# The first modulation's partial sum on VectorE: its place among the differences, and five blocks instead of four

## The chip, the core and the metric

The kernel runs on one core of one Trainium2 chip. A core has TensorE (PE: matmuls, with weight loads listed as PEld), VectorE (DVE), ScalarE (ACT), GpSimd (POOL) and SyncE (SP), which issues most of the transfers. Each has its own queue of instructions, which it takes in order, and they meet at semaphores. The metric is the device time of one execution in microseconds (us), the median of several runs.

## What is computed

A trunk of two layers for one sequence of 2048 positions and 1024 channels, all in float32. What matters here is the front of layer 0, the modulation of the input and the first product:

```
cond = silu(c)                                   # (1, 1024)
mod = cond @ ada_w[0] + ada_b[0]                 # ada_w[0]: (1024, 3072)
shift, scale, gate = split(mod, 3)
u = x * (1 + scale) + shift                      # x: (2048, 1024)
a, g, z = split(u @ w_in + b_in, 3)              # then a gated convolution, a second
                                                 # product, and a residual LayerNorm
```

Layer 1 is built alike, with another mixer. The output is (1, 2048, 1024).

## The kernel before, in words

The sequence is cut into halves of 1024 positions, and each product of a half is made as two by two blocks by a Strassen-Winograd scheme: seven products of blocks instead of eight, for which differences of the blocks of `u` are needed: `t1` to `t4` beside the blocks `b11`, `b21`, `b22` themselves (`b12` enters only through differences). For accuracy each of these seven is kept as two tiles, a rounded one made by ScalarE (`...h`, line L219) and the rest that the rounding left (`...l`, L220), made by GpSimd, and for `t1` and `t4` by VectorE. The weights (`wa`, `wz`, from the raw blocks `rawa`, `rawz`) are split in the same way by ScalarE and GpSimd. A product is then three matmuls for each of four sets of channels.

The 1024 channels are handled as four **sets** of 2 x 128 channels at the start. The loop at L971 runs over them, i from 0 to 3 (and once more, for the last products). A set does the following:

- `modulation_a(i)` (L443) loads eight blocks of `ada_w`, 128 rows each, `adak` (j = 0 to 5, in `u` buffers) and `adal` (j = 6 and 7, in a `raw` buffer, of which there are four, shared with the raw weights). VectorE multiplies block 0 by its entry of `cond` (L456) and adds blocks 1 to 3 to it, one scalar_tensor_tensor each (L458): the **sum**. TensorE then makes the modulation `pm`: for each of four outputs, blocks 4 to 7 against `cond`, and at last the sum against a column of ones. VectorE adds the bias (L470, tile `mod`).
- `u_block` (four times) loads a block of `x` (`xkua`), TensorE transposes it (`ptxua`), and ScalarE applies scale and shift as it copies it out of PSUM (L236, tile `ufua`).
- `u_parts` makes the seven pairs of tiles. VectorE's part are four differences (L253) and the rests of `t1` and `t4`.
- `first_products` runs, with the set before, the four products that open the kernel's long sequence: three of weight pair 0, one of weight pair 1. After set 0 the first three parts of pair 0 are asked for.

Who goes first: a planner orders each engine's queue when the kernel is built, by priorities and its own estimate of times. Instructions in an `urgent` block have a high priority, others go by their place in the program. Two orders are fixed by hand: TensorE's instructions stay in program order (`keep_in_program_order` ties an instruction behind the one traced before it on its engine), and a load stays behind the last load of weights or of `ada_w` (chain "w") and of its own chain. VectorE's instructions are not tied. What follows the start, some 1600 us of it, is one sequence of products with convolution steps of VectorE and GpSimd laid between them.

Of the kernel before, what the change touches and what calls it, by code (L numbers as in the profile page):

```python
# [9 lines left out]
F32 = mybir.dt.float32  # L10
F32R = mybir.dt.float32r
AF = mybir.ActivationFunctionType
ALU = mybir.AluOpType
# [3 lines left out]
P = 128  # L17
D = 1024
S = 2048
K = D // P  # L20
KH = K // 2
# [18 lines left out]
def hybrid_trunk(ctx, tc, x, c, ada_w, ada_b, a_w_in, a_b_in, a_conv_w, a_conv_b,  # L40
# [7 lines left out]
    nc = tc.nc  # L48
# [7 lines left out]
    def st(tag, shape, name, dtype=F32):  # L56
        return sb.tile(shape, dtype, tag=tag, bufs=BUFS[tag], name=name)

    def bank(tag, name):
        return psum.tile([P, T], F32, tag=tag, bufs=BANKS[tag], name=name)  # L60
# [3 lines left out]
    def load(dst, src, chain="w"):  # L64


        with ExitStack() as order:
            for key in {"w", chain}:
                if key in chains:
                    order.enter_context(tc.issue_after(chains[key]))  # L70
            chains[chain] = nc.sync.dma_start(dst, src).ins
# [25 lines left out]
    def matmul(*args, **kw):  # L97
        return tc.keep_in_program_order(nc.tensor.matmul(*args, **kw))  # L98

    def transpose(*args):  # L100
        return tc.keep_in_program_order(nc.tensor.transpose(*args))  # L101

    clock = [0]
    waiting = []

# [6 lines left out]
    def tick(taps, *gens):  # L112
# [8 lines left out]
        for job in due:  # L121
# [5 lines left out]
    ones = const.tile([P, P], F32, name="ones")  # L127
# [10 lines left out]
    second = [("ada_b1", cols(ada_b[1]), 3 * K),  # L138
              ("b_in", cols(a_b_in[0]), 3 * K),
              ("conv_b", cols(a_conv_b[0]), K),  # L140
              ("ln_g", cols(a_ln_g[0]), K),
              ("ln_b", cols(a_ln_b[0]), K),
              ("post_g", cols(post_ln_g[0]), K),
              ("post_b", cols(post_ln_b[0]), K),
              ("wb", b_conv_w[0].rearrange("k (j p) -> (k j) p", p=P), KB * K)]
# [9 lines left out]
    rows_in = {}  # L155

    def load_rows(gi, g):
        rt = st("acc", [P, P], f"rt{gi}")
        o = 0
        for key, ap, m in g:  # L160
            load(rt[o:o + m, :], ap)
            o += m
        return rt
# [14 lines left out]
    cond = const.tile([P, K], F32, name="cond")  # L178
# [33 lines left out]
    quarters = lambda ap: ap.rearrange("(s m two) d -> s two m d", s=2, two=2)  # L212
# [4 lines left out]

    def split(src, hi, lo, eng=None):
        nc.scalar.copy(hi, src)  # L219
        (eng or nc.gpsimd).tensor_tensor(lo, src, hi.bitcast(F32), op=ALU.subtract)  # L220

    def u_tile(src, name, eng=None):
        hi = st("u", [P, T], name + "h", F32R)
        lo = st("u", [P, T], name + "l", F32R)
        split(src, hi, lo, eng)
        return hi, lo
# [3 lines left out]
    def u_columns(xk, hf, k, su, bu, name):  # L230
        pt = bank("tp", f"ptx{name}{hf}_{k}")
        for t in range(NT):
            transpose(pt[:, t * P:(t + 1) * P], xk[:, t], ident)
        f = st("uf", [P, T], f"uf{name}{hf}_{k}")
        with urgent():
            nc.scalar.activation(f, pt, AF.Identity, scale=su(k), bias=bu(k))  # L236
        return f

    def u_block(src, sc, hf, k, su, bu, name, tag):

        xk = st(tag, [P, NT, P], f"xk{name}{hf}_{k}")
        load(xk, quarters(src)[sc, hf][:, k * P:(k + 1) * P]
             .rearrange("(t p) j -> p t j", p=P), "u")
        return u_columns(xk, hf, k, su, bu, name)

    def u_first(U, fs, name):
        with urgent():
# [2 lines left out]

    def u_second(U, f0, f1, name):
        (b11, b21), (b12, b22) = f0, f1
        tt = lambda o, a, b: nc.vector.tensor_tensor(o, a, b, op=ALU.subtract)  # L253
        with urgent():
            tt(b11, b12, b11)
            U["t1"].append(u_tile(b11, name + "t1", nc.vector))
            U["b22"].append(u_tile(b22, name + "b22"))
            tt(b11, b22, b11)
            U["t2"].append(u_tile(b11, name + "t2"))
            tt(b12, b22, b12)  # L260
            U["t3"].append(u_tile(b12, name + "t3"))
            t4 = st("uf", [P, T], f"{name}t4")
            tt(t4, b21, b11)
            U["t4"].append(u_tile(t4, name + "t4", nc.vector))
# [151 lines left out]
    def product(pair, p, ks=range(KH)):  # L416
        for i in ks:
            pair.mm(p, i)
            if i == KH - 1:
                pair.evacuate(p)  # L420
# [15 lines left out]
    mod0 = const.tile([P, KH, 2, 2], F32, name="mod0")  # L436
    su0 = lambda k: mod0[:, k // 2, 1, k % 2:k % 2 + 1]
    bu0 = lambda k: mod0[:, k // 2, 0, k % 2:k % 2 + 1]
    ab0 = const.tile([P, 2, K], F32, name="ab0")
    nc.vector.tensor_copy(ab0[:, 0], col["ada_b0"][:, :K])  # L440
    nc.vector.tensor_scalar(ab0[:, 1], col["ada_b0"][:, K:2 * K], 1.0, None, op0=ALU.add)

    def modulation_a(i):  # L443

        pm = bank("conv", f"pm{i}")
        raws = []
        last = st("raw", [P, 2, 2, 2 * P], f"adal{i}")
        for j in range(K):
            raw = last[:, j - 6] if j > 5 else st("u", [P, 2, 2 * P], f"adak{i}_{j}")
            load(raw, ada_w[0, j * P:(j + 1) * P, :2 * D].rearrange("p (m d) -> p m d", m=2)  # L450
                 [:, :, 2 * i * P:(2 * i + 2) * P])
            raws.append(raw)

        acc = raws[0]
        with urgent():
            nc.vector.tensor_scalar(acc, acc, cond[:, :1], None, op0=ALU.mult)  # L456
            for j in range(1, 4):
                nc.vector.scalar_tensor_tensor(out=acc, in0=raws[j], scalar=cond[:, j:j + 1],  # L458
                                               in1=acc, op0=ALU.mult, op1=ALU.add)
        for m in range(2):  # L460
            for b in range(2):
                o = m * 2 + b
                for j in range(4, K):
                    matmul(pm[:, o:o + 1], raws[j][:, m, b * P:(b + 1) * P],
                           cond[:, j:j + 1], start=(j == 4), stop=False)
                matmul(pm[:, o:o + 1], acc[:, m, b * P:(b + 1) * P], ones[:, :1],
                       start=False, stop=True)
        with urgent():
            for m in range(2):
                nc.vector.tensor_tensor(mod0[:, i, m], pm[:, 2 * m:2 * m + 2],  # L470
                                        ab0[:, m, 2 * i:2 * i + 2], op=ALU.add)

    sh1 = const.tile([P, K], F32, name="sh1")
    sc1 = const.tile([P, K], F32, name="sc1")
# [482 lines left out]
    def u_parts(U, f0, f1, name):  # L957
        u_first(U, f0, name)
        u_second(U, f0, f1, name)
# [6 lines left out]
    def first_products(pairs, ks):  # L966
        for k in ks:
            for p, r in early:
                product(pairs[p], r, [k])

    for i in range(KH + 1):  # L971
        if i < KH:
            if i == 2:
                rows_in[1] = load_rows(1, second)
            if i == 3:
                rows_in[2] = load_rows(2, taps_1)
                rows_in[3] = load_rows(3, taps_2)
            modulation_a(i)
            fs = [[u_block(x, 0, hf, 2 * i + b, su0, bu0, "ua0", "ta") for b in range(2)]
                  for hf in range(2)]  # L980
            u_parts(US[0, 0], *fs, f"ua0{i}")
        if i == 0:
            for p in (1, 2, 5):
                pa[0][0].part(p)
        if i == 3:
            load_columns(1, second, second_columns)
            nc.vector.tensor_scalar(half_b[:, 0], col["b_in"][:, :K], 0.5, None, op0=ALU.mult)
            nc.vector.tensor_scalar(half_b[:, 1], col["b_in"][:, K:2 * K], 0.5, None,
                                    op0=ALU.mult)
            nc.vector.tensor_scalar(negb, col["conv_b"], -1.0, None, op0=ALU.mult)  # L990
        if i == 4:
            tap_tables()
        if i:
            first_products(pa[0], [i - 1])

    def slowly(gen, ticks=2):
        due = 0
        for _ in gen:
            due += ticks
            while due >= 1:  # L1000
                yield
                due -= 1
# [31 lines left out]
    def second_u():  # L1034

        for i in range(KH):
            f0, f1 = [], []
            for b in range(2):
                for hf, fs in ((0, f0), (1, f1)):
                    fs.append(u_block(x, 1, hf, 2 * i + b, su0, bu0, "ua1", "xk"))  # L1040
                    if hf == 0 or b == 0:
                        yield
            u_parts(US[0, 1], f0, f1, f"ua1{i}")
            yield
# [9 lines left out]
    for n, (p, r) in enumerate(order_a):  # L1054
# [5 lines left out]
        if (p, r) in ((late_b, 3), (late_a, 4)):  # L1060
            k = 0 if r == 3 else 1
# [45 lines left out]
    def ending(pairs, order, rate, q, *beside):  # L1107
# [12 lines left out]
        for gen in gens:  # L1120
            for _ in gen:
# [12 lines left out]
    start = [(0, 1), (0, 2), (1, 1), (1, 2), (2, 1), (2, 2), (0, 5), (0, 6), (0, 3), (0, 7),  # L1134
             (1, 5), (0, 4), (1, 6)]
# [63 lines left out]
```

## Time and profile before

| | |
|---|---|
| median of three runs | 1720.44 us |
| lowest and highest | 1716.67 and 1728.08 us |
| the profiled execution, its own time | 1725.78 us |
| its span on the core | 1724.0 us |
| TensorE busy in the span | 1578.9 us (92%) |
| VectorE, GpSimd, ScalarE busy | 1165.1, 956.8, 665.9 us |

The profile is one execution. Times in it count from the start of the span. A row of the instructions in order of time has start, duration, engine, line, operation, output and inputs; "x3" says that three went into the row, and the bracket at its end says how long the engine had stood idle before it and who ended that. The granted clock of TensorE is given as a share of its full clock: 1.00 is 2.4 GHz and 0.50 is 1.2 GHz.

### The profile page before, as it was taken

To read this page: it belongs to the slowest core of one execution; us is meant where nothing else is said; L and a number is where in the kernel's file an instruction comes from. 1 tells how busy PE (TensorE), PEld (TensorE's weight loads), DVE (VectorE), ACT (ScalarE), POOL (GpSimd) and SP (SyncE) were. 2 spreads that over 40 slices of the span, in tenths; PEclk is the share of its full clock that TensorE was granted. 3 is DMA by queue.
4 is the path that set the end of the run, shared out by engine and by line. 5 is a ranking of instruction groups with operands and counts; after the bars stand their busy time and mean duration, and the time that the engine had idled before them with its cause. 6 is when DMAs were issued, how large, how long until landed. Compare 5 with 4: busy or idle time off the path is not lost.

```text
span 1724.0 us, 20944 instructions
## 1 busy us (share of the span) xinstructions
PE 1578.9 (92%) x6860; PEld 1278.1 (74%) x6860; DVE 1165.1 (68%) x1816; ACT 665.9 (39%) x1134; POOL 956.8 (56%) x808
## 2 busy tenths in 40 slices
PE   4699999889999989868999999898899999999996
PEld 3577787668888767656777887677688888878885
DVE  4438999997899887997999963564832222226555
ACT  2345444655533335373444333333732221112221
POOL 4368886965656343866888776727565541121110
PEclk9799999899999989988999999899899999999998
DMA  7358888779999997634777667986688887787995
GB/s 221 114 198 295 293 298 322 228 276 391 333 354 363 357 368 257 208 147 166 265 266 255 245 245 286 342 289 223 220 294 282 306 298 221 229 299 260 329 336 222
DMA packets 237916, 469.64 MB, mean 272 GB/s; under 512 B 20328, under 2 KB 102640, under 8 KB 237808
## 3 DMA queue, kind: packets, MB, share of 16 engines
q1 hardware_dynamic: 190864, 323.06, 55.6%
q10 hardware_dynamic: 46944, 145.25, 21.7%
q8 instruction: 55, 0.90, 0.2%
q14 instruction: 53, 0.43, 0.1%
HBM read 297.72 MB, written 170.52 MB: 272 GB/s over the span
## 4 chain that ended last, share of the span: by engine, by line
PE 59%; DVE 18%; DMA 11%; issue 4%; POOL 3%; ACT 3%; SPq 1%; ACTq 0%; DVEq 0%; POOLq 0%
PE po L98 17%; PE pxb L98 7%; PE pxc L98 7%; PE pxa L98 5%; PE pzb L98 4%; DVE pca L555 4%; PE pzc L98 4%; PE pza L98 3%; DVE pcb L555 3%; DMA keptb<-wb 3%; PE pxz L98 2%; DMA wr<-w_dram 2%; DMA kepta<-wa 2%; PE pya L98 2%; PE pyb L98 2%
## 5 line engine op out<-in xcount | busy, mean ns | idle before, releaser
L555 DVE SCALAR_TENSOR_TENSOR pcb<-h,w,pcb 128x512 f32<-128x512 f32 x224 | 166.7, 744 | 8.4 <-ACT pcb L563 8.0
L555 DVE SCALAR_TENSOR_TENSOR pca<-h,w,pca 128x512 f32<-128x512 f32 x192 | 142.8, 744 | 0.2
L555 DVE SCALAR_TENSOR_TENSOR pca<-xs,w,pca 128x512 f32<-128x512 f32 x128 | 95.5, 746 | 0.8
L825 DVE TENSOR_TENSOR r<-po,r 128x512 f32<-128x512 f32 x64 | 43.3, 683 | 70.0 <-PE po L98 31.6
L555 DVE SCALAR_TENSOR_TENSOR pcd<-xs,w,pcd 128x512 f32<-128x512 f32 x112 | 83.4, 745 | 0.1
L500 POOL TENSOR_TENSOR ada<-ada,adaw 128x512 f32<-128x512 f32 x48 | 63.9, 1331 | 35.1 <-ACT adaw L494 16.0
L795 ACT ACTIVATE r<-r,nb,rs 128x512 f32<-128x512 f32 x64 | 47.3, 808 | 80.4 <-DVE nb L792 80.3
L220 POOL TENSOR_TENSOR gb_0l<-vb,gb_0h 128x512 fp32r<-128x512 f32 x4 | 5.2, 1295 | 110.2 <-ACT gb_0h L219 110.2
L530 POOL TENSOR_TENSOR wf<-wf,grow 128x512 f32<-128x512 f32 x32 | 41.9, 1318 | 37.6 <-DMA wf<-in_b_w_out_dram 33.6
L832 POOL TENSOR_TENSOR rs<-rs,mhalf 128x1 f32<-128x1 f32 x32 | 18.3, 584 | 75.6 <-DVE rs L831 75.6
L220 POOL TENSOR_TENSOR wa<-rawa,wa 128x512 fp32r<-128x512 f32 x32 | 43.2, 1352 | 21.2 <-ACT wa L219 21.0
L569 POOL TENSOR_TENSOR lead<-lead,part 128x512 f32<-128x512 f32 x32 | 43.6, 1362 | 19.8 <-ACT part L568 17.3
L220 POOL TENSOR_TENSOR wc<-rawc,wc 128x512 fp32r<-128x512 f32 x32 | 46.0, 1437 | 15.5 <-ACT wc L219 15.3
L894 POOL TENSOR_TENSOR hb1c<-c12c,c22c 128x512 f32<-128x512 f32 x16 | 21.1, 1322 | 59.1 <-DVE c22c L392 54.8
L220 POOL TENSOR_TENSOR wf<-wf 128x512 fp32r<-128x512 f32 x32 | 43.0, 1351 | 18.4 <-ACT wf L219 13.7
L804 DVE TENSOR_TENSOR r<-r,g 128x512 f32<-128x512 f32 x48 | 39.6, 838 | 20.0 <-PE ptx L101 17.5
L786 POOL TENSOR_TENSOR r<-r,gb 128x512 f32<-128x512 f32 x32 | 43.9, 1388 | 15.7 <-DMA r<-in_x_dram 14.4
L817 ACT ACTIVATE ub<-ptx,post_sh,post_sc 128x128 f32<-128x128 f32 x128 | 47.0, 482 | 13.4 <-PE ptx L101 13.4
L494 ACT ACTIVATE adaw<-adaw,cond 128x512 f32<-128x512 f32 x64 | 42.5, 715 | 24.8 <-DMA adaw<-in_ada_w_dram 24.3
L220 POOL TENSOR_TENSOR wb<-rawb,wb 128x512 fp32r<-128x512 f32 x32 | 45.2, 1412 | 7.6 <-ACT wb L219 7.4
L220 POOL TENSOR_TENSOR wb<-sb,wb 128x512 fp32r<-128x512 f32 x24 | 35.4, 1473 | 25.0 <-ACT wb L219 25.0
L739 ACT ACTIVATE v<-v,second_columns 128x512 f32<-128x512 f32 x32 | 25.9, 814 | 55.0 <-DVE v L738 53.8
(1388 smaller groups left out, 5589.2 us busy)
## 6 DMA issues: line engine op xcount, KB each, us to landing
wr<-w_dram SPq DMA_DIRECT2D x128, 512.0 KB
kepta<-wa ACTq DMA_DIRECT2D x56, 512.0 KB
wa<-kepta SPq DMA_DIRECT2D x56, 512.0 KB
keptc<-wc ACTq DMA_DIRECT2D x56, 512.0 KB
keptb<-wb ACTq DMA_DIRECT2D x56, 512.0 KB
wc<-keptc SPq DMA_DIRECT2D x56, 512.0 KB
wb<-keptb SPq DMA_DIRECT2D x56, 512.0 KB
adaw<-in_ada_w_dram SPq DMA_DIRECT2D x32, 512.0 KB
```

Source lines behind the costliest of these rows:

```text
L98: return tc.keep_in_program_order(nc.tensor.matmul(*args, **kw))
L220: (eng or nc.gpsimd).tensor_tensor(lo, src, hi.bitcast(F32), op=ALU.subtract)
L494: nc.scalar.activation(raw[:, j], raw[:, j], AF.Identity, scale=cond[:, kk + j:kk + j + 1])
L500: nc.gpsimd.tensor_tensor(acc, acc, raw[:, j], op=ALU.add)
L530: nc.gpsimd.tensor_tensor(w[:, 1], w[:, 1], grow, op=ALU.mult)
L555: nc.vector.scalar_tensor_tensor(out=tiles[out], in0=src, scalar=w, in1=tiles[acc], op0=ALU.mult, op1=op)
L569: nc.gpsimd.tensor_tensor(lead, lead, part, op=ALU.add)
L786: nc.gpsimd.tensor_tensor(rt, rt, gb[0][h], op=ALU.add)
L795: nc.scalar.activation(rts[t, h], rts[t, h], AF.Identity, scale=rs, bias=nb)
L804: eng.tensor_tensor(r, r, g[h], op=ALU.mult)
L817: nc.scalar.activation(fs[k][:, t * P:(t + 1) * P], pt[:, j * P:(j + 1) * P], AF.Identity, scale=post_sc[:, k:k + 1], bias=post_sh[:, k:k ...
L825: nc.vector.tensor_tensor(r, pss[t], r, op=ALU.add)
```

## The change

The loads and the sum of a set leave `modulation_a` for a function of their own, `modulation_loads`. Set 0's is called ahead of the loop; in trip i of the loop, the loads and the sum of set i+1 come after the modulation of set i and the loads of its `x` blocks, and in front of the transposes, copies and differences of set i. While `starting` holds, VectorE's instructions of the sum, the modulation, the differences and the rests of `t1` and `t4` are tied in program order (`pinned`). So VectorE's order becomes: modulation i, sum i+1, differences i, modulation i+1. The sum takes five blocks instead of four (`SPLIT`), and TensorE's part three instead of four. As the loads of set i+1 are now asked for before the weights that follow set i in the program, they also go ahead of these in SyncE's queue. The small row loads (`second`, `taps_1`, `taps_2`) move with them by one trip.

```diff
+    def pinned(made):
+        return tc.keep_in_program_order(made) if starting[0] else made
+
+    starting = [True]
...
     def split(src, hi, lo, eng=None):
         nc.scalar.copy(hi, src)
-        (eng or nc.gpsimd).tensor_tensor(lo, src, hi.bitcast(F32), op=ALU.subtract)
+        made = (eng or nc.gpsimd).tensor_tensor(lo, src, hi.bitcast(F32), op=ALU.subtract)
+        if eng is nc.vector:
+            pinned(made)
...
-    def u_block(src, sc, hf, k, su, bu, name, tag):
+    def x_block(sc, hf, k, name, tag):
 
         xk = st(tag, [P, NT, P], f"xk{name}{hf}_{k}")
-        load(xk, quarters(src)[sc, hf][:, k * P:(k + 1) * P]
+        load(xk, quarters(x)[sc, hf][:, k * P:(k + 1) * P]
              .rearrange("(t p) j -> p t j", p=P), "u")
-        return u_columns(xk, hf, k, su, bu, name)
+        return xk
+
+    def u_block(sc, hf, k, su, bu, name, tag):
+
+        return u_columns(x_block(sc, hf, k, name, tag), hf, k, su, bu, name)
...
-        tt = lambda o, a, b: nc.vector.tensor_tensor(o, a, b, op=ALU.subtract)
+        tt = lambda o, a, b: pinned(nc.vector.tensor_tensor(o, a, b, op=ALU.subtract))
...
-    def modulation_a(i):
-
-        pm = bank("conv", f"pm{i}")
+    SPLIT = 5
+
+    def modulation_loads(i):
+
         raws = []
...
         acc = raws[0]
         with urgent():
-            nc.vector.tensor_scalar(acc, acc, cond[:, :1], None, op0=ALU.mult)
-            for j in range(1, 4):
-                nc.vector.scalar_tensor_tensor(out=acc, in0=raws[j], scalar=cond[:, j:j + 1],
-                                               in1=acc, op0=ALU.mult, op1=ALU.add)
+            pinned(nc.vector.tensor_scalar(acc, acc, cond[:, :1], None, op0=ALU.mult))
+            for j in range(1, SPLIT):
+                pinned(nc.vector.scalar_tensor_tensor(out=acc, in0=raws[j],
+                                                      scalar=cond[:, j:j + 1], in1=acc,
+                                                      op0=ALU.mult, op1=ALU.add))
+        return raws
+
+    def modulation_a(i, raws):
+
+        pm = bank("conv", f"pm{i}")
         for m in range(2):
             for b in range(2):
                 o = m * 2 + b
-                for j in range(4, K):
+                for j in range(SPLIT, K):
                     matmul(pm[:, o:o + 1], raws[j][:, m, b * P:(b + 1) * P],
-                           cond[:, j:j + 1], start=(j == 4), stop=False)
-                matmul(pm[:, o:o + 1], acc[:, m, b * P:(b + 1) * P], ones[:, :1],
+                           cond[:, j:j + 1], start=(j == SPLIT), stop=False)
+                matmul(pm[:, o:o + 1], raws[0][:, m, b * P:(b + 1) * P], ones[:, :1],
                        start=False, stop=True)
         with urgent():
             for m in range(2):
-                nc.vector.tensor_tensor(mod0[:, i, m], pm[:, 2 * m:2 * m + 2],
-                                        ab0[:, m, 2 * i:2 * i + 2], op=ALU.add)
+                pinned(nc.vector.tensor_tensor(mod0[:, i, m], pm[:, 2 * m:2 * m + 2],
+                                               ab0[:, m, 2 * i:2 * i + 2], op=ALU.add))
...
+    raws = modulation_loads(0)
     for i in range(KH + 1):
         if i < KH:
+            modulation_a(i, raws)
+            xs_ = [[x_block(0, hf, 2 * i + b, "ua0", "ta") for b in range(2)] for hf in range(2)]
+            if i == 1:
+                rows_in[1] = load_rows(1, second)
             if i == 2:
-                rows_in[1] = load_rows(1, second)
-            if i == 3:
                 rows_in[2] = load_rows(2, taps_1)
                 rows_in[3] = load_rows(3, taps_2)
-            modulation_a(i)
-            fs = [[u_block(x, 0, hf, 2 * i + b, su0, bu0, "ua0", "ta") for b in range(2)]
+            if i + 1 < KH:
+                raws = modulation_loads(i + 1)
+            fs = [[u_columns(xs_[hf][b], hf, 2 * i + b, su0, bu0, "ua0") for b in range(2)]
                   for hf in range(2)]
             u_parts(US[0, 0], *fs, f"ua0{i}")
...
+    starting[0] = False
```

## Rows read from the trace of the kernel before

**Rows 1.** The page: busy us, share of the span, instructions, of each engine.

```profile
PE 1578.9 (92%) x6860; PEld 1278.1 (74%) x6860; DVE 1165.1 (68%) x1816; ACT 665.9 (39%) x1134; POOL 956.8 (56%) x808
```

**Rows 2.** Busy time by stage: stretch, its length, engines, granted clock, DMA share, GB/s.

```profile
39.60:46.30 6.70, 6.65 (x32) 6.65 (x33) 0.00 (x0) 0.00 (x0) 0.00 (x0) 1.00 0.01 2
...
61.70:68.30 6.60, 6.58 (x31) 6.58 (x32) 0.00 (x0) 0.00 (x0) 0.00 (x0) 0.50 0.00 0
...
76.80:83.60 6.80, 0.02 (x1) 0.00 (x0) 5.66 (x7) 1.66 (x3) 2.94 (x2) 0.75 0.01 1
500.00:900.00 400.00, 356.77 (x1512) 281.79 (x1511) 354.51 (x556) 170.26 (x303) 239.24 (x200) 0.94 0.75 270
```

**Rows 3.** Waits in the first 100 us: total us, times, longest us.

```profile
PE pm L98 <- DVE adak L458: 29.1, 3, 14.5
```

**Rows 4.** VectorE's instructions of the first 110 us in order of time.

```profile
18.75 0.23 DVE L470 TENSOR_TENSOR mod<-pm,ab 128x2 f32<-128x2 f32 x2 [10.09 <-PE pm L98]
23.91 3.41 DVE L253 TENSOR_TENSOR ufua<-ufua,ufua 128x512 f32<-128x512 f32 x2 [4.93 <-POOL ua00b11l L220]
...
32.37 0.82 DVE L220 TENSOR_TENSOR ua00t4l<-ua00t,ua00t4h 128x512 fp32r<-128x512 f32 x1 [1.00 <-ACT ua00t4h L219]
33.11 1.48 DVE L456 TENSOR_SCALAR adak<-adak,cond 128x512 f32<-128x512 f32 x1
34.63 4.97 DVE L458 SCALAR_TENSOR_TENSOR adak<-adak,cond,adak 128x512 f32<-128x512 f32 x3
46.67 0.23 DVE L470 TENSOR_TENSOR mod<-pm,ab 128x2 f32<-128x2 f32 x2 [7.08 <-PE pm L98]
...
59.34 2.33 DVE L458 SCALAR_TENSOR_TENSOR adak<-adak,cond,adak 128x512 f32<-128x512 f32 x3
68.74 0.23 DVE L470 TENSOR_TENSOR mod<-pm,ab 128x2 f32<-128x2 f32 x2 [7.08 <-PE pm L98]
72.62 0.69 DVE L253 TENSOR_TENSOR ufua<-ufua,ufua 128x512 f32<-128x512 f32 x1 [3.65 <-ACT ufua L236]
...
79.03 0.82 DVE L220 TENSOR_TENSOR ua02t4l<-ua02t,ua02t4h 128x512 fp32r<-128x512 f32 x1 [1.00 <-ACT ua02t4h L219]
...
90.69 0.23 DVE L470 TENSOR_TENSOR mod<-pm,ab 128x2 f32<-128x2 f32 x2 [7.08 <-PE pm L98]
```

**Rows 5.** The chain of waits, first 160 us: start, us, what.

```profile
39.65 6.98 PE pm L98 x32
...
61.72 6.99 PE pm L98 x32
```

**Rows 6.** TensorE's instructions in order of time, 40 to 80 us.

```profile
50.21 0.48 PE L98 MATMUL pxa<-ua00b11h,wa 128*128 128x512 f32 x1
...
53.03 0.50 PE L98 MATMUL pm<-cond,adak 128*128 128x1 f32 x4
...
72.67 0.78 PE L98 MATMUL pxa<-ua01b11h,wa 128*128 128x512 f32 x1
...
75.88 0.50 PE L98 MATMUL pm<-cond,adak 128*128 128x1 f32 x4
```

**Rows 7.** SyncE's transfers of the first 110 us, as issued, in order of time.

```profile
9.72 3.13 SPq L71 DMA_DIRECT2D rawa<-in_a_w_in_dram  x2
...
16.97 1.33 SPq L71 DMA_DIRECT2D adal<-in_ada_w_dram  x2
...
29.52 2.94 SPq L71 DMA_DIRECT2D adak<-in_ada_w_dram  x6
46.24 0.88 SPq L71 DMA_DIRECT2D adal<-in_ada_w_dram  x2
...
51.50 3.47 SPq L71 DMA_DIRECT2D adak<-in_ada_w_dram  x6
```

**Rows 8.** ScalarE's first cast of weights, and one of GpSimd's rests, from their timelines.

```profile
16.24 1.14 ACT L219 CAST wa<-rawa 128x512 fp32r<-128x512 f32 x2 [12.56 <-DMA rawa<-in_a_w_in_dram]
...
34.27 1.44 POOL L220 TENSOR_TENSOR wa<-rawa,wa 128x512 fp32r<-128x512 f32 x1
```

More of the change, by code (lines that the diff above doesn't have):

```diff
@@ L1039, in second_u @@
                 for hf, fs in ((0, f0), (1, f1)):
-                    fs.append(u_block(x, 1, hf, 2 * i + b, su0, bu0, "ua1", "xk"))
+                    fs.append(u_block(1, hf, 2 * i + b, su0, bu0, "ua1", "xk"))
                     if hf == 0 or b == 0:
```

## The prediction

> **What bounds the kernel now.** I read the shares of the page first: TensorE is busy 92% of the span, so over most of the kernel there is nothing that VectorE's order could win; only a stretch in which TensorE stands still can pay [rows 1]. Next, the busy time by stage: in 76.8 to 83.6 us TensorE does 0.02 us of work while VectorE does 5.66; the start is where it stands [rows 2]. Then the list of waits over the first 100 us: TensorE waits three times, 29.1 us together, for VectorE's sum `adak` of L458, and 14.5 us of that is one wait [rows 3]. This 29.1 us is the most that taking the wait away can give directly.
>
> Why the sum is late is read from VectorE's instructions in order of time [rows 4]. For sets 1, 2 and 3 the sum stands behind everything that the set before needs. Set 0: modulation done at 18.75, first difference 23.91, last rest `t4l` ends at 33.19 (32.37 + 0.82), and only then the sum of set 1 runs, 33.11 to 39.60. Sets 2 and 3 repeat it: `t4l` of set 2 at 79.03, the sum after it, modulation 3 at 90.69. TensorE has the matmuls of the sum in front of everything else in its own fixed order, so a loop forms: sum, 6.98 us of modulation matmuls [rows 5], modulation, transposes and copies, differences, rests, next sum. One trip takes 22.07 us (46.67 to 68.74) and 21.95 us (68.74 to 90.69) [rows 4].
>
> Between the modulation and the first difference VectorE does nothing (68.97 to 72.62): it waits for ScalarE's copies [rows 4]. That gap is where the sum goes.
>
> **The change, part by part.**
>
> *Five blocks on VectorE.* Each set gets one more scalar_tensor_tensor there. Uncontended it is 0.78 us (2.33 for three [rows 4]), contended 1.66 (4.97 for three [rows 4]). TensorE loses, for each of four outputs, one matmul, which the profile counts as two instructions: 40 become 32 in a set. The 32 instructions that now follow the wait take 6.98 us [rows 5], 0.218 each, so a whole set costs 6.98 from now on. Eight of the 40 ran beside the wait, so this part alone wins little in rounds 1 to 3; what it adds is that the whole group now starts unhindered. In set 0 three outputs lie behind the last landed block: 3 x 2 x 0.218 = 1.3 us earlier, modulation 0 at 17.4 instead of 18.75.
>
> *The sum in front of the differences.* In round 2 the sum would begin at the modulation + 0.25, and last 1.48 + 4 x 0.78 = 4.6 us at the contended price of its first instruction (VectorE's other first instructions in rounds 1 to 3 all took 1.48; the one of set 1 stands in [rows 4]). It ends at + 4.85; the differences could start at + 3.9 (72.62 - 68.74). So they go 1 us later. From the first difference to the end of `t4l` is 7.2 us (72.62 to 79.85) [rows 4]: VectorE would be through at + 12.1.
>
> *What is late next.* TensorE. From the end of the modulation matmuls to the first product of the set before: 68.71 to 72.67, 4.0 us; the 12 products to the next modulation matmul: 72.67 to 75.88, 3.2 [rows 5, 6]. With 6.98 that is a round of 14.2 us, above VectorE's 12.1. In round 1, whose modulation matmuls ran at a granted clock of 1.00 instead of 0.50, the same two pieces took 3.6 (46.63 to 50.21) and 2.8 (50.21 to 53.03) [rows 2, 5, 6], which gives 13.4. The modulation matmuls themselves take 6.98 at 1.00 and 6.99 at 0.50 [rows 2, 5]; whatever the clock does, I count at most 0.8 us a round for it. I take 14.2 and keep 13.4 for the range.
>
> *SyncE's queue.* The loads of set i+1 are still behind the x blocks of set i, as they were, and the row loads of `second` and of the taps keep their places too. What moves is two sets of weights. Pair 0's raw blocks, issued at 9.72, go behind set 1's eight loads, which were all out at 18.30 (16.97 + 1.33 [rows 7]); without the 3.13 us of the weights themselves that is 15.2. The first was used 6.5 us after issue (ScalarE's cast at 16.24 [rows 8]), now about 21.7. Nothing on TensorE needs them before the first products, near 36. But their work on GpSimd (1.44 us for one rest [rows 8]) now falls entirely beside set 0's differences, so I leave these at the contended 9.3 us (23.91 to 33.19), not 7.2. Set 1's sum needs its blocks by 17.4: issued from 9.72 on, they land at latest like the weights did, 16.2 for the first, so it ends near 21, before the first difference.
>
> Pair 1's first raw block goes from in front of set 2's loads (29.52 [rows 7]) to behind them, and needs a `raw` buffer, which set 1 frees as its matmuls end, near 32. Add 6.5 for landing, 0.6 for the cast (1.14 for two), and 1.7 for a rest that meets VectorE (my estimate, 1.44 and a little) [rows 8]: 40.8. TensorE wants it at modulation 1 + 4.0 + 2.4. This is a new wait, counted below; queued behind it are the remaining products of set 0 and all matmuls of set 2.
>
> *VectorE's new wait.* If a block of set i+1 has not landed, the sum stands, and behind it the differences of set i and then modulation i+1. Blocks of set 3 are behind set 2's last pair of blocks and its x blocks. In the trace the pair went out at 46.24, set 3's six from 51.50 to 54.97 [rows 7]; with 6.5 to land this is 15.2 us after the pair at most, against a round of 14.2. The pair waited then for set 1's buffer; with pair 1's weights now asked for later, set 0's buffer is free for it. I take no wait, up to 1 us on the upper side.
>
> *The sum.* Modulation 1: first difference at 17.4 + 5.2 (23.91 - 18.75) = 22.6, + 9.3 = 31.9, since it stands behind `t4l` in VectorE's order; TensorE's matmuls would be done by 29. Before: 46.67, so 14.8 earlier. Modulation 2: 31.9 + 14.2 + 2.6, the wait for pair 1 (40.8 less 38.3, rounded up) = 48.7. Modulation 3: + 14.2 = 62.9, against 90.69. That is **27.8 us**. After it the work is the same as before, product by product, and nothing in it keeps to a clock on the wall, so I move it whole: 1725.78 (span 1724.0 and 1.78 around it) becomes 1698.0. The profiled execution lies 5.3 above the median of three, 1720.44; from the median it is **1692.6**.
>
> Bounds: with uncontended differences (29.8) and two rounds of 13.4, modulation 3 is at 56.6, a gain of 34.1, 1686.3. The other end is the first rival.
>
> **A rule that speaks against it.** VectorE's instruction with two inputs took 1.66 us instead of 0.78 while GpSimd worked [rows 4, 8]. The Trainium skill, page "SBUF — State Buffer", section "SBUF: two separate sides", says why: the two engines arbitrate for one port pair, an exclusive lock held for the whole instruction, and a VectorE instruction with two SBUF inputs needs it. The trace agrees in kind, with 0.9 us lost. By the rule every one of the moved instructions can be blocked as soon as GpSimd is never idle, and the loop becomes VectorE's: that is rival 1.
>
> **Rivals.**
>
> 1. *VectorE becomes the bound.* Rounds shorten, so GpSimd's rests and weights fill all the time, and everything on VectorE runs contended: 0.23 + 1.48 + 4 x 1.66 + 9.3 = 17.6 a round, over TensorE's 14.2. Modulation 3 at 31.9 + 35.2 = 67.1, a gain of 23.6, 1696.8; with pair 1's weights 5 us later as well 1701.8. For it: set 0 looked like this. Against it: GpSimd did no work in 61.7 to 68.3 [rows 2]; there is room.
>
> 2. *The loads become the bound.* Only round 0 is saved, and in rounds 1 and 2 the sum stands for blocks of `ada_w`, with the differences behind it, until a round is 22 again. Gain 14.8, 1705.6. It takes blocks some 7 us later than the 15.2 above. For it: SyncE's queue stands behind a buffer from 32.46 to 46.24 (29.52 + 2.94 [rows 7]). Against it: that buffer comes free as the round shortens.
>
> 3. *Slower.* Only VectorE's and TensorE's order at the start is held; the rest is planned anew, and VectorE's order in 500 to 900 us is a delicate one: 354.5 of 400 us busy, TensorE 356.8, that is 43.2 us idle [rows 2]. If taps there go in front of the additions that free TensorE's banks, its idle time grows. From 71 us idle in this stretch all is lost, at 88 the time is 1737. Against it: the order in that stretch comes from the program's steps and priorities, which the change leaves alone.
>
> 4. *It does not do what it says.* The wait for the sum turns into the same wait for transposes or x blocks: 1720, no change. Against it: those blocks are issued a round ahead of their use.
>
> **How the numbers follow.** Forecast 0.62 at 1692.6, its own range 1686 to 1697. Rival 1: 0.20; rival 2: 0.09; rival 3: 0.05; rival 4: 0.04. A measurement of this kernel, whose three runs spread from 1716.67 to 1728.08, tells about 1% (17 us) from no change. Faster by more than that: forecast and rival 1, 0.82; within it, rivals 2 and 4, 0.13; slower, 0.05. The range reaches from the best bound less 2 for the scatter, 1684, to rival 2's time, 1706.
>
> **What would show it.** In the changed profile: VectorE's `adak` sum right behind each `mod`, five instructions, before the differences; no idle of TensorE put down to L458 over 1 us; `mod` at about 17, 32, 49 and 63 us; pair 1's weights as the one new wait on TensorE. Wrong would be: VectorE idle in front of L458 for a load (rival 2), scalar_tensor_tensor at 1.6 us throughout (rival 1), or a start that is shorter by 28 us and an end that is not (rival 3).

## The result, and the profile after

The changed kernel takes **1701.46 us** (median; 1698.88 to 1706.84 in 4 runs) against 1720.78 (1716.67 to 1728.08, 4 runs): a ratio of 0.9881, interval 0.9848 to 0.9915. That is 1.2% faster, by 19.3 us, inside the whole range (1684 to 1706), above the forecast's own range (1686 to 1697) and above the likeliest time of 1692.6 by 8.9. The execution shown below took 1698.88 us, its span 1696.8; the one of before took 1725.78. Between these two the difference is 26.9.

The engines' line of the page (busy time, share of the span, instructions), for [rows 1]:

```profile
PE 1568.5 (92%) x6828; PEld 1267.6 (75%) x6828; DVE 1171.5 (69%) x1820; ACT 665.7 (39%) x1134; POOL 963.8 (57%) x808
```

The shares are within a point of what they were. What changed is the list of TensorE's waits, here over the first 100 us (engine, output and line, what it waited for: us, times, longest):

```profile
PE pm L98 <- DMA adak<-in_ada_w_dram: 6.6, 1, 6.6
PE pxa L98 <- ACT wa L224: 5.8, 1, 5.8
PE ptxua L101 <- ACT ufua L243: 5.2, 4, 3.2
...
PE pxa L98 <- POOL wa L225: 1.3, 1, 1.3
```

The wait for the sum, 29.1 us in three pieces [rows 3], is gone. In its place stand 5.8 + 1.3 us for pair 1's first weight, which ScalarE rounds (L224) and GpSimd takes the rest of (L225). The first row is the wait for the first blocks at the very start, which before has too. The third is longer than it was; the kernel before had

```profile
PE ptxua L101 <- ACT ufua L236: 1.5, 4, 0.9
```

The transposes wait for ScalarE's copies (L243), and in rounds 1 and 3 these now wait for `mod`, which is late on VectorE.

VectorE's instructions in order of time, for [rows 4]:

```profile
17.40 0.23 DVE L487 TENSOR_TENSOR mod<-pm,ab 128x2 f32<-128x2 f32 x2 [7.52 <-PE pm L98]
17.54 0.48 DVE L467 TENSOR_SCALAR adak<-adak,cond 128x512 f32<-128x512 f32 x1
18.05 4.01 DVE L469 SCALAR_TENSOR_TENSOR adak<-adak,cond,adak 128x512 f32<-128x512 f32 x4
21.99 1.75 DVE L264 TENSOR_TENSOR ufua<-ufua,ufua 128x512 f32<-128x512 f32 x1
...
31.15 0.99 DVE L225 TENSOR_TENSOR ua00t4l<-ua00t,ua00t4h 128x512 fp32r<-128x512 f32 x1 [0.68 <-ACT ua00t4h L224]
32.07 0.21 DVE L487 TENSOR_TENSOR mod<-pm,ab 128x2 f32<-128x2 f32 x2
32.20 1.34 DVE L467 TENSOR_SCALAR adak<-adak,cond 128x512 f32<-128x512 f32 x1
33.59 6.71 DVE L469 SCALAR_TENSOR_TENSOR adak<-adak,cond,adak 128x512 f32<-128x512 f32 x4
40.22 1.75 DVE L264 TENSOR_TENSOR ufua<-ufua,ufua 128x512 f32<-128x512 f32 x1
...
49.07 0.99 DVE L225 TENSOR_TENSOR ua01t4l<-ua01t,ua01t4h 128x512 fp32r<-128x512 f32 x1 [0.69 <-ACT ua01t4h L224]
53.66 0.22 DVE L487 TENSOR_TENSOR mod<-pm,ab 128x2 f32<-128x2 f32 x2 [3.60 <-PE pm L98]
53.80 0.47 DVE L467 TENSOR_SCALAR adak<-adak,cond 128x512 f32<-128x512 f32 x1
54.31 4.01 DVE L469 SCALAR_TENSOR_TENSOR adak<-adak,cond,adak 128x512 f32<-128x512 f32 x4
...
64.97 1.00 DVE L225 TENSOR_TENSOR ua02t4l<-ua02t,ua02t4h 128x512 fp32r<-128x512 f32 x1 [0.68 <-ACT ua02t4h L224]
65.89 0.21 DVE L487 TENSOR_TENSOR mod<-pm,ab 128x2 f32<-128x2 f32 x2
```

Each `mod` is now followed at once by five instructions of the next sum. A `mod` with no bracket at its end (32.07, 65.89) waited for nothing: VectorE itself was late. The one at 53.66 waited 3.60 us for TensorE. So rounds 0 and 2 are set by VectorE, round 1 by TensorE with VectorE 3.6 us behind it. The four scalar_tensor_tensors of set 2 (33.59) take 1.68 us each; those of sets 1 and 3 take 1.00.

TensorE in round 1, and the two engines that it waits for (start, us, and in brackets the idle time before):

```profile
43.70 0.79 PE L98 MATMUL pxa<-ua00b11h,wa 128*128 128x512 f32 x1 [5.82 <-ACT wa L224]
...
46.20 0.80 PE L98 MATMUL pxa<-ua00b11h,wa 128*128 128x512 f32 x1 [1.28 <-POOL wa L225]
...
75.77 0.50 PE L98 MATMUL pxa<-ua00t2h,wa 128*128 128x512 f32 x1
```

```profile
41.99 0.62 ACT L224 CAST ua01t1h<-ufua 128x512 fp32r<-128x512 f32 x1 [5.61 <-DVE ufua L264]
...
43.04 0.61 ACT L224 CAST wa<-rawa 128x512 fp32r<-128x512 f32 x1
...
31.81 0.41 SPq L71 DMA_DIRECT2D rawa<-in_a_w_in_dram  x1
...
39.71 1.71 POOL L361 TENSOR_TENSOR rawa<-rawa,rawa 128x512 f32<-128x512 f32 x1
...
44.44 1.72 POOL L225 TENSOR_TENSOR wa<-rawa,wa 128x512 fp32r<-128x512 f32 x1
51.15 1.27 POOL L359 TENSOR_TENSOR sa<-rawa,sa 128x512 f32<-128x512 f32 x1
```

Pair 1's raw weights are asked for at 31.81, as forecast (near 32). Their cast starts at 43.04. ScalarE stood idle for 5.61 us up to 41.99: the cast of `t1` is ahead of that of the weights in its queue, and `t1` is the first difference on VectorE (40.22), which now stands behind the slow sum. So the sum that was moved still holds TensorE, by another way: sum, difference, cast of `t1`, cast of weights, product.

The last row of the TensorE fence is the first product with `t2`, where the start ends: 75.77 us. Before has it at 101.43, so the start became 25.7 us shorter; modulation 3 came 24.8 earlier (65.89 against 90.69 [rows 4]). In the kernel before:

```profile
101.43 0.50 PE L98 MATMUL pxa<-ua00t2h,wa 128*128 128x512 f32 x1 [1.04 <-ACT c11a L387]
```

The granted clock by stretch (us; busy time and count of TensorE, its weight loads, VectorE, ScalarE, GpSimd; then the clock, the share of the DMA engines and GB/s), for [rows 2]:

```profile
21.40:28.10 6.70, 6.70 (x34) 6.70 (x33) 5.98 (x5) 4.14 (x8) 6.50 (x5) 1.00 0.87 211
...
38.00:39.50 1.50, 0.00 (x0) 0.00 (x0) 1.46 (x2) 0.00 (x0) 1.50 (x2) 1.00 1.13 291
39.50:41.00 1.50, 0.00 (x0) 0.00 (x0) 1.50 (x2) 0.00 (x0) 1.50 (x2) 0.62 1.00 283
...
46.80:53.50 6.70, 6.70 (x34) 6.70 (x32) 2.57 (x2) 1.17 (x2) 5.62 (x4) 0.50 0.01 4
...
60.10:63.60 3.50, 3.50 (x34) 3.50 (x32) 2.86 (x3) 1.58 (x3) 1.26 (x1) 1.00 0.13 16
```

The modulation matmuls of set 2 take 6.7 us at 0.50 (1.2 GHz), the same ones of set 3 take 3.5 at 1.00 (2.4 GHz). Those of set 1 take 6.7 at a recorded 1.00. (Each of these three stretches is busy throughout; two of the 34 instructions are neighbours of the set's 32.)

### The profile page after: what moved, and what is told of

The parts are those of the page before. It is cut to its first block, busy times and chain, and to the rows that moved or that the text cites. A ratio compares the mean times of both kernels' runs of the same rounds, so it can differ in the third digit from the quotient of the medians.

```text
span 1696.8 us, 20882 instructions
## 1 busy us (share of the span) xinstructions
PE 1568.5 (92%) x6828; PEld 1267.6 (75%) x6828; DVE 1171.5 (69%) x1820; ACT 665.7 (39%) x1134; POOL 963.8 (57%) x808
## 4 chain that ended last, share of the span: by engine, by line
PE 52%; DVE 21%; DMA 12%; POOL 7%; issue 5%; ACT 2%; ACTq 0%; SPq 0%; DVEq 0%; POOLq 0%
PE po L98 19%; PE pxb L98 6%; PE pxc L98 6%; DVE pca L572 5%; PE pxa L98 4%; DVE pcb L572 4%; PE pzb L98 3%; DMA keptb<-wb 3%; PE pzc L98 3%; DMA keptc<-wc 2%; PE pza L98 2%; PE pxz L98 2%; DMA wr<-w_dram 2%; PE pyc L98 1%; DVE pcd L572 1%
## 5 line engine op out<-in xcount | busy, mean ns | idle before, releaser
L225 POOL TENSOR_TENSOR gb_0l<-vb,gb_0h 128x512 fp32r<-128x512 f32 x4 | 5.2, 1292 | 111.2 <-ACT gb_0h L224 111.2
L225 POOL TENSOR_TENSOR wc<-rawc,wc 128x512 fp32r<-128x512 f32 x32 | 45.1, 1409 | 16.8 <-ACT wc L224 16.7
L225 POOL TENSOR_TENSOR wf<-wf 128x512 fp32r<-128x512 f32 x32 | 42.9, 1350 | 17.6 <-ACT wf L224 17.6
L225 POOL TENSOR_TENSOR wb<-sb,wb 128x512 fp32r<-128x512 f32 x24 | 35.3, 1473 | 23.7 <-ACT wb L224 23.7
L225 POOL TENSOR_TENSOR wb<-rawb,wb 128x512 fp32r<-128x512 f32 x32 | 44.7, 1398 | 6.3 <-ACT wb L224 4.0
L225 POOL TENSOR_TENSOR wa<-rawa,wa 128x512 fp32r<-128x512 f32 x32 | 44.9, 1407 | 4.0 <-ACT wa L224 2.4
```

The lines of the kernel that those rows point to most:

```text
L225: made = (eng or nc.gpsimd).tensor_tensor(lo, src, hi.bitcast(F32), op=ALU.subtract)
```

## The experiments

**Theory:** the place of the sum in VectorE's queue makes the gain; the rounds are then set by VectorE beside GpSimd, and in round 1 by pair 1's weights. **Rivals:** the fifth block makes part of it; the earlier loads make it; the weights or their queue cost the missing microseconds. Each kernel is compared with the kernel before, run beside it; e1 to e12 are the names of the runs. "t2" is the start of the first product with `t2` in the run's profile.

**What the comparison can tell.** The change again (e1), and the kernel before against itself (e12), both without edits:

> The change once more, in more rounds, as the measure for the parts. The start's theory (the start is shorter and everything behind it moves whole): the modulation of set 3 stands 24.8 us earlier and the first t2 product 25.7 earlier in the two profiles, so the gain is 23 to 27 us, ratio 0.984 to 0.987. Rival (part of the gain is lost again behind the start): 19 us or less, ratio 0.989 or more, and the profile shows TensorE idle longer than before at 100 us and later.

> The kernel before against itself: what the comparison shows of no change, and a second profile of its start. Ratio 0.998 to 1.002. If the profile shown of before is typical: first t2 product at 101 to 102, and 4 to 5 us of the start's gain are missing in the medians. If that profile had a late start: near 99, as in the run with the split alone, and 2 to 3 us of those were never there.

Measured: the change 1700.62 us (1697.13 to 1702.68, 6 runs), ratio 0.9884 [0.9864, 0.9903], t2 at 76.75. Before against itself: 0.9991 [0.9972, 1.0011], t2 at 101.95. The gain is there again, 20.8 us. It lies between the two expectations: short of the 23 to 27 us of a start that moves everything behind it whole, a little over the 19 of its rival. The profile shown of before had a usual start, so the missing microseconds are not a late start of that one profile.

**The split alone** (e3, the kernel before with five blocks):

```
-            for j in range(1, 4):
+            for j in range(1, 5):
...
-                for j in range(4, K):
+                for j in range(5, K):
...
```

> The kernel before with five blocks on VectorE and nothing else. The place theory: about no change; set 0 wins 1.3 us, and in each of three rounds the sum is 0.75 to 1.7 us later while TensorE has the same 32 instructions behind it: 1 to 4 us slower than before. If the fifth block pays by itself: 5 us or more faster.

Measured: 1720.25 us (12 runs), 0.9994 [0.9975, 1.0013]. It was expected to be 1 to 4 us slower and is not. Its profile has t2 at 98.96, some 2.5 to 3 us before the two profiles of before, which the median doesn't show; and the wait for the sum is still there:

```profile
PE pm L98 <- DVE adak L458: 31.3, 3, 14.6
```

**The order alone** (e2, the change with `SPLIT = 4`):

> The change with four blocks on VectorE, as before. If the place of the sum is what pays: within 4 us of the whole change, since VectorE's sum is one instruction shorter (0.75 to 1.7 us a round) and TensorE's group 8 instructions longer (0.9 to 1.75 us). If the fifth block carries a good part of it: 6 us or more slower than the whole change.

Measured: 1699.77 us (1693.85 to 1701.23, 5 runs), 0.9871 [0.985, 0.9893], t2 at 76.43. Together with the split alone: the fifth block brings nothing that the medians can measure in either order (the intervals reach 0.2% to either side); it brings modulation 0 forward from 18.16 to 17.40 and puts one more instruction of 1.7 us on VectorE in round 1.

**The loads alone** (e4; loads as in the change; the sum back in `modulation_a`, four blocks, nothing tied on VectorE):

```
-    starting = [True]
+    starting = [False]
...
+        return raws
+
+    def modulation_a(i, raws):
+
+        pm = bank("conv", f"pm{i}")
         acc = raws[0]
         with urgent():
             pinned(nc.vector.tensor_scalar(acc, acc, cond[:, :1], None, op0=ALU.mult))
...
```

> The loads of the next set ahead, as in the change; the sum stays in the modulation's function, four blocks, nothing pinned on VectorE. If the tie on VectorE is needed: TensorE's three waits for the sum stay and the time is that of before within 5 us. If the place of the loads in SyncE's queue decides and the planner pulls the sum forward by itself once its blocks are there: 15 to 25 us faster than before, with the sum in front of most differences in the profile.

Measured: 1701.20 us (1699.94 to 1705.05, 6 runs), 0.989 [0.9871, 0.9908], t2 at 75.77: all of the gain. VectorE's order tells why:

```profile
15.97 2.33 DVE L474 SCALAR_TENSOR_TENSOR adak<-adak,cond,adak 128x512 f32<-128x512 f32 x3 [0.33 <-DMA adak<-in_ada_w_dram]
18.60 0.23 DVE L487 TENSOR_TENSOR mod<-pm,ab 128x2 f32<-128x2 f32 x2 [0.30 <-PE pm L98]
...
33.19 1.48 DVE L472 TENSOR_SCALAR adak<-adak,cond 128x512 f32<-128x512 f32 x1
34.59 0.21 DVE L487 TENSOR_TENSOR mod<-pm,ab 128x2 f32<-128x2 f32 x2
34.73 4.98 DVE L474 SCALAR_TENSOR_TENSOR adak<-adak,cond,adak 128x512 f32<-128x512 f32 x3
```

With its blocks asked for earlier, the planner put the sum in front of the differences by itself, around `mod` 0 and `mod` 1. So the ties on VectorE are not needed where the blocks are early. Whether the early blocks or the place of the sum makes the gain, this run leaves open: it has both.

**The early loads with the sum behind** (e11, the change, but the sum is traced, and tied, behind the differences):

```
+    def modulation_sum(raws):
...
             u_parts(US[0, 0], *fs, f"ua0{i}")
+            if i + 1 < KH:
+                modulation_sum(raws)
...
```

> The change with one thing undone: the sum for the next set is tied behind this set's differences on VectorE; its blocks are asked for as early as in the change. If the place of the sum on VectorE makes the gain: the sum starts where t4l ends, near 31, takes up to 8.0 us beside GpSimd, and pm follows with some 6 us, so mods at about 17.4 / 45 / 67 / 89, the first t2 product near 98, median 1716 to 1721. If the early blocks make it: mods as in the change (32 / 54 / 66), median 1700 to 1702.

Measured: 1724.75 us (1720.33 to 1733.31, 12 runs), 1.0017 [0.9998, 1.0037]; t2 at 102.46. Nothing is left of the gain (the median is even above the expected 1716 to 1721), and the wait for the sum is longer than in before:

```profile
PE pm L98 <- DVE adak L473: 36.4, 3, 17.1
```

```profile
30.53 0.98 DVE L225 TENSOR_TENSOR ua00t4l<-ua00t,ua00t4h 128x512 fp32r<-128x512 f32 x1 [0.69 <-ACT ua00t4h L224]
31.44 1.48 DVE L471 TENSOR_SCALAR adak<-adak,cond 128x512 f32<-128x512 f32 x1
32.96 5.75 DVE L473 SCALAR_TENSOR_TENSOR adak<-adak,cond,adak 128x512 f32<-128x512 f32 x4
44.51 0.23 DVE L490 TENSOR_TENSOR mod<-pm,ab 128x2 f32<-128x2 f32 x2 [5.80 <-PE pm L98]
```

The sum starts where `t4l` ends, and `mod` 1 comes at 44.51 (45 expected). This pair of runs shows the cause: the early blocks alone give nothing, the place of the sum on VectorE is the gain. Whether a tied sum needs the early blocks as well is answered by e7 below.

**The wait for pair 1's weights.** Four kernels take it away or alter it. First, the cast of the weights tied ahead of the cast of `t1` on ScalarE, twice with five blocks (e5, e10) and once with four (e9, `SPLIT = 4`). `pin_cast` ties the next cast, that of `t1`, behind the one traced just before it:

```
         u_first(U, f0, name)
+        if name == "ua01":
+            with urgent():
+                pa[0][1].part(1)
+            pin_cast[0] = True
         u_second(U, f0, f1, name)
```

> The change, with ScalarE's cast of pair 1's first weights tied in front of its cast of set 1's t1 (before it stood behind two casts that wait for VectorE's differences). If TensorE's wait of 4.8 to 5.8 us in the round of set 1 is ScalarE's queue, behind VectorE's contended sum: the product of pair 1 comes 3 us earlier, near 43 instead of 46.2, and modulation 2 goes from 53.7 to 50 or 51, which is where VectorE's own chain ends; the whole is 2 to 4 us faster than the change. If the weights had landed late: the cast starts at 42 or later as before, nothing changes.

> The run with the cast ahead once more, beside the one with four blocks. If the gain over the change is real: median 1696 to 1699, mod 2 near 50.7, wait for pair 1's first weight under 2 us. If it was the scatter of its runs: 1700 to 1702.

> Four blocks on VectorE with the cast of pair 1's first weight ahead of set 1's t1 cast. If the fifth block is worth nothing and the cast is a small gain: mods at about 17.5 / 32.5 / 51 / 63.5, the first t2 product near 73.5, median 1697 to 1699. If VectorE's sum sets the round 1 to 2 once the weights are early, taking a block of 1.7 us from that sum shows: mod 2 at 49, median 1 to 2 us under the run with five blocks.

Measured: 1697.13 us (1691.38 to 1705.44, 5 runs) and 1702.26 (1700.09 to 1708.18, 6 runs); with four blocks 1695.13 (1692.27 to 1697.62, 4 runs), 0.9852 [0.9828, 0.9876]. The eleven runs of the first kernel together have a median of 1700.77; the change had 1701.46 and 1700.62. So the lower median of the first five isn't a gain. The profiles of this kernel are alike: t2 at 73.61 and 73.29, some 2.5 us before the change's. From the second:

```profile
38.93 0.62 ACT L225 CAST wa<-rawa 128x512 fp32r<-128x512 f32 x1 [2.44 <-DMA rawa<-in_a_w_in_dram]
```

```profile
49.45 0.99 DVE L229 TENSOR_TENSOR ua01t4l<-ua01t,ua01t4h 128x512 fp32r<-128x512 f32 x1 [0.69 <-ACT ua01t4h L225]
50.36 0.21 DVE L491 TENSOR_TENSOR mod<-pm,ab 128x2 f32<-128x2 f32 x2
```

The cast waits for its data alone, 4 us earlier than in the change, and `mod` 2 comes right behind VectorE's `t4l`. TensorE still waits 4.2 us for this weight in e10 (2.9 of it for GpSimd's rest; under 2 was expected), but that no longer counts. So of the 7.1 us on TensorE 3 to 4 could be won and no more: VectorE stands next. The total doesn't show the start that is 2.5 us shorter; the intervals reach some 3.4 us to either side. The run with four blocks is the lowest whole kernel here: its four runs lie below all six of e10, measured beside it. Yet its t2 stands at 75.09, later than e10's 73.29, so its lead would come from behind the start; the kernel of e10 itself had 1697.13 in e5; and its interval overlaps that of the change. It isn't claimed to be better, and the question is open.

Second (e6), pair 1's product with set 0 moved behind set 1, so that TensorE needs the weights one round later:

```
+                if (p, r) == (1, 1) and starting[0] and k < 2:
+                    pairs[p].part(r)
+                    if k == 1:
+                        product(pairs[p], r, [0, 1])
```

> The change, with the product of set 0 and pair 1's first weights made one set later, so that TensorE doesn't want these weights in the round of set 1. If TensorE's wait set the length of this round alone: modulation 2 near 46 to 47, the start 6 to 7 us shorter. If VectorE's chain stands right behind it (its last rest of set 1 ended at 50.06): modulation 2 at 50 to 51 with no wait for TensorE, the start 2 to 4 us shorter.

Measured: 1701.17 us (1697.74 to 1706.17, 4 runs), 0.9885 [0.9865, 0.9905]; t2 at 73.47. No wait for pair 1's first weight is left, and `mod` 2 again stands right behind `t4l`, 17.9 us after `mod` 1 (31.93):

```profile
48.93 0.99 DVE L225 TENSOR_TENSOR ua01t4l<-ua01t,ua01t4h 128x512 fp32r<-128x512 f32 x1 [0.68 <-ACT ua01t4h L224]
49.84 0.21 DVE L487 TENSOR_TENSOR mod<-pm,ab 128x2 f32<-128x2 f32 x2
```

Third (e7), the raw weights of pairs 0 and 1 asked for ahead of the next set's blocks:

```
+            if i == 0:
+                for p in (1, 2, 5):
+                    pa[0][0].part(p)
+            if i == 1:
+                pa[0][1].part(1)
             if i + 1 < KH:
                 raws = modulation_loads(i + 1)
```

> The change, with the raw weights of pair 0 and pair 1 asked for ahead of the next set's blocks, as before. Contention theory: GpSimd does pair 0's work earlier, the sum of set 1 waits 2 to 4 us for its blocks, and modulation 1 comes at 33 to 35, but the round of set 1 is shorter, with less of GpSimd's work in it: modulation 3 at 63 to 66, the time within 3 us of the change. If the weights' place in the queue is what paid: modulation 1 at 38 or later and a time 6 us or more above the change.

Measured: 1702.30 us (1701.9 to 1706.91, 4 runs), 0.9895 [0.9879, 0.9912]; t2 at 74.77. No wait for pair 1's first weight is left, but modulation 1 slips from 32.07 to 36.61: the sum of set 1 waits 0.97 us for its blocks, and beside GpSimd's earlier rests its four instructions take 6.65 us instead of 4.01. Round 1 then takes 14.7 us (to a `mod` 2 at 51.30) instead of 21.6. So modulation 3 is 1.7 us earlier (64.19), and the total is no shorter.

This run also answers the question that e11 left. SyncE asks in the order of before, for pair 0's weights first, and for set 1's blocks later than before did (12.90):

```profile
9.93 3.47 SPq L71 DMA_DIRECT2D rawa<-in_a_w_in_dram  x2
13.44 4.00 SPq L71 DMA_DIRECT2D adak<-in_ada_w_dram  x6
```

The gain is there all the same. So a sum that is tied in its place doesn't need the early blocks; they matter where nothing is tied and the planner chooses the place (e4).

**GpSimd beside VectorE** (e8). The rests of the weights that are made during the start are left out (GpSimd writes zeros in their place, so part of the product is missing):

```
+                if starting[0]:
+                    nc.scalar.copy(wt[:, 0], src)
+                    nc.gpsimd.memset(wt[:, 1].bitcast(F32), 0.0)
+                else:
+                    split(src, wt[:, 0], wt[:, 1])
```

> The change, leaving out the rests of the weights that are made during the start (a memset of zeros by GpSimd instead of the subtraction that reads two inputs). If the length of the round of set 1 is VectorE's contention with GpSimd: its scalar_tensor_tensor go from 1.68 us towards 0.75, the chain from modulation 1 to the last rest from 18.0 to 13 to 15 us, modulation 3 at 58 to 62. If the round is bound by TensorE's wait for loads: modulation 2 stays at 52 to 54.

Measured: 1696.31 us (1693.7 to 1700.25, 4 runs), 0.9856 [0.9839, 0.9874]; t2 at 70.72, 5.0 us before the change's. VectorE's chain of round 1, from `mod` to the end of `t4l`, takes 16.0 us (30.46 to 46.50) instead of 18.0 (32.07 to 50.06):

```profile
30.46 0.21 DVE L491 TENSOR_TENSOR mod<-pm,ab 128x2 f32<-128x2 f32 x2
...
31.98 5.82 DVE L473 SCALAR_TENSOR_TENSOR adak<-adak,cond,adak 128x512 f32<-128x512 f32 x4
...
45.51 0.99 DVE L225 TENSOR_TENSOR ua01t4l<-ua01t,ua01t4h 128x512 fp32r<-128x512 f32 x1 [0.68 <-ACT ua01t4h L224]
```

GpSimd's rests thus lengthen VectorE's chain, by 2 us in this round; 13 to 15 us were expected of it, but the rests of the columns remain and still stretch the sum to 1.46 us a piece. `mod` 2 comes at 48.44, after 1.94 us of waiting for TensorE, so here TensorE sets round 1 again.

## Why the prediction was right, and where it was off

**The mechanism was right.** The three waits for the sum are gone, the place of the sum on VectorE makes the gain (e2, e7, e11), and the largest new wait on TensorE is the forecast one, pair 1's weights. It isn't the only one: the transposes' wait for ScalarE's copies grew from 1.5 to 5.2 us. Rivals 2 and 4 didn't come: none of the sums of sets 1 to 3 stood for its blocks, and the wait for the sum didn't become an equal wait for something else.

**Round 0: right, in part by luck.** Modulations 0 and 1 at 17.40 and 32.07, against 17.4 and 31.9. The gain of round 0 is 14.6 of 14.8. But the first difference came at 21.99 instead of 22.6, and from there to the end of `t4l` it took 10.15 us instead of 9.3; the two nearly cancel.

**Round 1: mis-sized, by 4.8 us** (21.6 instead of 16.8). The step "the wait for pair 1 (40.8 less 38.3)" failed: it was 7.1 us on TensorE instead of 2.6. The prediction counted issue, landing, cast and rest as if each engine were free. The landing was near its estimate (6.5; in e10 the cast, waiting for data alone, starts 6.9 us after the issue at 32.04), but on ScalarE the cast stood behind that of `t1`. SyncE's and GpSimd's queues were followed, and ScalarE's was not. Then TensorE, idle from 37.9, lost its clock: 1.00 until 39.5, 0.50 in the stretch from 46.8, and the modulation matmuls of set 2 took 6.7 us at that. Of all this 3.6 us lay on the path, since VectorE's chain was nearly as late.

**Rival 1 held for this round.** Its formula (everything on VectorE contended) gives 17.6 us; the chain measured 18.0, and with the weights out of the way the round is 17.9 (e6). Its time with the weights late, 1701.8, is also the time that was measured, but not by its reasons alone: in rounds 0 and 2 the sum ran at 1.00 us a piece, not at 1.66. That the total met this time is luck.

**Round 2: mis-sized the other way, by 2.0 us** (12.2 instead of 14.2). The step "whatever the clock does, I count at most 0.8 us a round" failed. It rested on 6.98 us at a recorded 1.00 and 6.99 at 0.50. But a row shown there spoke against it: four modulation matmuls in 0.50 us at 53.03 [rows 6] are 0.125 us each, against 0.218. Here the set took 3.5 us at 1.00. TensorE's round then would be some 10 us, and VectorE's 12.1, worked out in the prediction, became the bound: `mod` 3 follows `t4l` without a wait. Its sum took 4.5 us against 4.6, by another split: 0.47 for the first instruction and 4.01 for four, not 1.48 and 3.12.

**The sum.** Rounds 1 and 2 together make the start's gain 24.8 us at modulation 3 (25.7 at t2) instead of 27.8. That explains 3 of the 8.9 us. The measured time lies in the stretch of the range that was added for rivals 1 and 2, not in the forecast's own.

**The rest of the 8.9 us: "I move it whole" is not borne out by the medians.** For each kernel, the median less t2 of its profile is the time behind the start. The four kernels with a long start (before, e3, e11, e12) have 1618.3 to 1622.3, mean 1620.3; the ten with a short one 1620.0 to 1629.0, mean 1625.2. So about 5 us of the start's gain is given back later. In the profiles the first product `po` comes on average 512.8 us behind t2 in the four and 512.3 in the ten (514.0 and 512.7 in the two shown): up to about 590 us the gain is whole. From there to the end of the span the two groups differ by 3.7 us, but single profiles of one group scatter by about 4 (standard deviation), so the place isn't settled. Rival 3 (VectorE's order behind the start) may be at work in small, but no run tests it. The two executions profiled first happen to differ by 26.9 us; the medians are the better measure.

**The fifth block, the ties:** the first was said to win little, and wins nothing that the medians show. That the ties might not be needed had not been considered.

**A rule weighed again.** Beside GpSimd the four scalar_tensor_tensors of set 2 took 6.71 us, and GpSimd's own instructions in that stretch 1.71 to 1.73 each, against 1.27 with VectorE idle (51.15). The Trainium skill, page "SBUF — State Buffer", section "SBUF: two separate sides", calls the shared ports an exclusive lock for the whole instruction. Strictly one after the other, a pair would take 0.78 + 1.27 = 2.05 us; measured are 1.7. Both engines lose, as the rule says, but part of their work overlaps.

## What to carry to other kernels

When a wait is taken away, follow what is queued behind it on every engine, the quiet ones too: here ScalarE, 39% busy, carried the moved delay from VectorE to TensorE. Before a chain on one engine is called shorter than the next bound, price that bound at the clock that the shorter stalls will give it, and check the price against every row that shows the same instruction. Here the order on one engine came about by tying it and also, untied, by asking for its data earlier; a run that forces the order back with the early data kept, and one that keeps the order with the data late, tell which of the two pays.

## What the runs showed of the hardware

**A recorded clock of 1.00 at the start isn't the rate.** Up to its first change the record stands at 1.00, whatever the matmuls do. In the kernel before it does so through an idle stretch of TensorE from 25 to 39.65 us and the modulation matmuls behind it (0.21 us each, 39.60 to 46.30 [rows 2]); up to 39 us:

```profile
0.00:39.00 39.00, 14.97 (x65) 13.76 (x65) 17.39 (x21) 11.00 (x18) 20.97 (x25) 1.00 0.83 244
```

In the changed kernel the modulation matmuls of set 1 take 0.21 us each at this 1.00 (6.68 for 32, from 21.43 us), just as those of set 2 at 0.50; in e1 the same matmuls take 0.12 each, also at a recorded 1.00 (3.73 for 32, from 21.72 us; the record falls as they end). The level can be read only after the record has first changed; until then the durations tell it.

**Small matmuls follow the clock.** Matmuls with a single column (128x1), of which the profile counts two instructions each, take half the time at twice the clock: 6.7 us at 0.50 in the stretch from 46.8, 3.5 at 1.00 in the one from 60.1. The weight loads (PEld) are busy through the whole of both stretches.
